# Fifteen low weight parts of the first mixer on GpSimd instead of VectorE

## The chip, the cores and the metric

One NeuronCore of a Trainium2 chip runs the whole program in one launch. The metric is device time in microseconds (us), the median over timed executions; lower is better. One further execution was taken by the hardware profiler, and all durations below come from that one. The engines are TensorE (PE, with its weight loads as PEld), VectorE (DVE), ScalarE (ACT), GpSimd (POOL) and SyncE (SP), each with its own instruction queue that runs strictly in order.

## What is computed

Two transformer-like blocks in fp32 on 256 tokens of width 1024, batch 1. The change concerns the first half of the first block, here called the first mixer:

```python
def first_block(x, ...):
    xn = rms_norm(x, norm1_w)
    z = xn @ w_in                       # q, k_c, v_c, k_s, v_s, k_w, v_w, g_nsa, xr, gr, g_a, g_b
    attn = nsa_attention(q, ...)        # compressed, selected and windowed keys, three softmaxes
    rnn = rg_lru_branch(xr, gr, ...)    # conv of 4, gated linear recurrence
    merged = sigmoid(g_a) * (attn @ w_up_attn) + sigmoid(g_b) * (rnn @ w_up_rnn)
    x = x + merged @ w_out
    hn = rms_norm(x, norm2_w)
    x = x + square(relu(hn @ mlp_w1)) @ mlp_w2
    return rms_norm(x, final_norm_w)

def compress_blocks(k, pos, w1, w2):    # k_c and v_c, blocks of 32 tokens with stride 16
    ...
    return gelu(flat @ w1) @ w2
```

The second block is a SwiGLU, a mixer with two attentions, and a second SwiGLU.

## The kernel before, in words

**Weights in pieces.** All weights lie in one DRAM tensor in the order of use. A piece is up to 1024 columns of 128 partitions (the first eight: 512). Two pieces make a chunk, which one DMA on the SP queue loads into a `raw` buffer (three buffers, `load_to`, L227 to L241). To keep fp32 accuracy with TensorE's fp32r format, each piece is split: ACT copies it to `whi`, rounded to fp32r (L253), and DVE subtracts, `wlo = raw - whi` (L254). `whi` and `wlo` have five buffers each. `wt` (L258) calls for a piece's split when the piece two ahead of it is needed. Each product of TensorE then takes three matmuls: `whi` with the high and the low part of the activations, and `wlo` with the high part (L305, L299).

Each buffer comes free when its last reader is done: a `raw` buffer when both `whi` and both `wlo` of its chunk are made, a `whi` or `wlo` buffer when TensorE has used it.

**What sets the order.** The code records steps in the order of `ORDER_1` (L156). A scheduler then places the instructions of each engine by its own estimate of durations and of what is ready; the result is a fixed list for every engine. An edit of one instruction's engine can thus change the lists of all engines.

**Pieces of the first mixer.** Pieces 0 to 68 belong to it: `q`, `k`, `xr`, `vg`, the gates `ga`, `gb`, `gr`, the compression weights `cw1` (pieces 16, 17, 18, 22, 23, 24, 27, 28), the recurrence `lru`, and the two merges `m1b` and `m1a`. From piece 69 on comes `wo`, the output projection. Names used below:

- `Sn`: attention scores (L825, L826), from `q` and from `k`, whose low part for the other half of the partitions is an ACT copy (L589).
- `cmpA`: the rows of `k_c` and `v_c`, shifted, written by four DMAs that GpSimd issues (L569, L570), first the two of group 0 and then the two of group 1. `cmpB` is their high and low part: eight ACT copies (L334) and eight DVE subtractions (L335), four for each group. `cmph` is the product of `cmpB` and the compression weights (L674); its first half needs four of the eight, two of each group.
- `vg`: values and gates (L299), first with piece 19.
- GpSimd's other work in this stretch is `rnn_prep`, a chain of some 25 operations on 128x8 elements (L886 to L905, a series for softplus), and `rs_A` (L476), the reciprocal root of the first norm.
- `rnn`: the recurrence's output in two parts, high by ACT (L334) and low by DVE (L335), which `m1b` multiplies (L305).

Of the kernel before, what the change touches and what calls it, by code (L numbers as in the profile page):

```python
# [8 lines left out]
F32 = mybir.dt.float32  # L9
F32R = mybir.dt.float32r  # L10
AF = mybir.ActivationFunctionType
ALU = mybir.AluOpType
# [11 lines left out]
EARLY = 8  # L24
# [164 lines left out]
class Prog:  # L189
# [15 lines left out]
    def prepare(self):  # L205
        self.chunks = self.plan.chunks()
        self.chunk_of = {}
        self.off = []
        o = 0
        for ci, ch in enumerate(self.chunks):  # L210
            w = sum(self.plan.pieces[i][0] for i in ch)
            self.off.append((o, w))
            o += P * w
            x = 0
            for i in ch:
                self.chunk_of[i] = (ci, x)
                x += self.plan.pieces[i][0]
        self.total = o
        self.raw = {}
        self.split = {}  # L220
        self.n_dma = 0
        self.n_split = 0
        self.hi_ins = []
        self.lo_ins = []
        self.raw_ins = []
# [17 lines left out]
    def split_to(self, i):  # L243
        nc = self.nc
        while self.n_split <= min(i, len(self.plan.pieces) - 1):
            p = self.n_split
            ci, x = self.chunk_of[p]
            self.load_to(ci + 2 if ci >= EARLY else max(ci + 2, EARLY))
            w = self.plan.pieces[p][0]
            src = self.raw[ci][:, x:x + w]  # L250
            hi = self.pools["whi"].tile([P, PIECE], F32R, tag="whi", name=f"whi{p}")
            lo = self.pools["wlo"].tile([P, PIECE], F32R, tag="wlo", name=f"wlo{p}")
            self.hi_ins.append(nc.scalar.activation(out=hi[:, :w], in_=src, func=AF.Copy))  # L253
            self.lo_ins.append(nc.vector.tensor_tensor(out=lo[:, :w], in0=src, in1=hi[:, :w].bitcast(F32), op=ALU.subtract))  # L254
            self.split[p] = (hi, lo)
            self.n_split += 1

# [1342 lines left out]
```

## Time and profile before

| what | value |
|---|---|
| median of 3 runs | 966.38 us (965.74 to 966.56) |
| profiled execution, its own time | 965.97 us |
| its span, first to last instruction | 964.2 us |
| instructions | 15723 |
| share of busy time | PE 98%, PEld 90%, DVE 75%, ACT 61%, POOL 4% |

The profiled execution lies 0.41 us below the median, and its span 1.8 us below its own time. A busy share is a mean over the whole program. What ends the idle time of an engine stands in brackets in a timeline's rows, and a row with a count (x2) merges instructions of the same kind that follow each other, so its time runs from the first start to the last end. The ends of matmuls are modelled: rows of PE overlap, and what counts is when the next one starts.

### The profile page before, as it was taken

The page shows a single profiled execution, that of the slowest core. Times are in us where ns is not written, and L with a number is a line of the kernel's source. Part 1 is how long each engine was busy: PE and PEld are TensorE (multiplying, and loading weights), DVE is VectorE, ACT ScalarE, POOL GpSimd, SP SyncE. Part 2 cuts the span into 40 slices and gives each one's busy share as a digit, 9 for nine tenths or more (in the row PEclk, how much of TensorE's full clock was granted, in tenths as well). Part 3 has the DMA queues.
Part 4 walks back from the last instruction along what each step waited for, and adds up shares of the span by engine and source line. Part 5 has one row for each costly group of instructions (what it writes and reads, how often), then busy time and mean ns, then how long its engine had stood idle before and what let it go on. Part 6 is the DMA issues. An engine that isn't in the chain of part 4 may idle for free.

```text
span 964.2 us, 15723 instructions
## 1 busy us (share of the span) xinstructions
PE 947.1 (98%) x6176; PEld 863.0 (90%) x6176; DVE 727.5 (75%) x1215; ACT 585.7 (61%) x962; POOL 36.6 (4%) x71
## 2 busy tenths in 40 slices
PE   7999999999999999999999999999999999999997
PEld 6989999998888888888888888999999888888885
DVE  6898879878887655579888666779776878878553
ACT  6695798546766544456555445588874566555541
POOL 1600000000000000020000200000000000000000
PEclk9999999999999999999999999999999999999999
DMA  8666333645555555556555755454333465554541
GB/s 302 218 229 250 130 135 132 228 139 185 180 198 190 175 181 201 186 189 196 197 193 178 234 189 178 142 196 140 124 123 141 175 233 182 189 204 173 179 159 44
DMA packets 27563, 174.01 MB, mean 180 GB/s; under 512 B 3425, under 2 KB 4705, under 8 KB 8289
## 3 DMA queue, kind: packets, MB, share of 16 engines
q1 hardware_dynamic: 25920, 169.60, 50.4%
q0 software_dynamic: 1136, 2.63, 1.2%
q8 instruction: 48, 0.79, 0.3%
q10 hardware_dynamic: 432, 0.79, 0.2%
q14 instruction: 27, 0.21, 0.1%
HBM read 171.43 MB, written 1.05 MB: 179 GB/s over the span
## 4 chain that ended last, share of the span: by engine, by line
PE 94%; ACT 3%; DVE 1%; issue 1%; DMA 1%; SPq 0%; POOLq 0%; POOL 0%; ACTq 0%; DVEq 0%
PE f L311 17%; PE w L311 12%; PE f L312 9%; PE w L312 6%; PE ld L299 6%; PE ga L305 5%; PE gb L305 5%; PE fd L311 4%; PE wo L311 3%; PE m1b L305 2%; PE gr L305 2%; PE fd L312 2%; PE xr L305 2%; PE wo L312 2%; PE qa L305 1%; PE m2b L305 1%
## 5 line engine op out<-in xcount | busy, mean ns | idle before, releaser
L254 DVE TENSOR_TENSOR wlo<-raw,whi 128x1024 fp32r<-128x1024 f32 (+2 forms) x324 | 388.7, 1203 | 167.2 <-ACT whi L253 147.6
L253 ACT ACTIVATE whi<-raw 128x1024 fp32r<-128x1024 f32 (+2 forms) x324 | 336.0, 1042 | 290.9 <-PE w L311 66.6
L311 PE MATMUL f<-u,whi 128*128 128x512 f32 x704 | 244.9, 393 | 0.0
L312 PE MATMUL f<-u,wlo 128*128 128x256 f32 x704 | 196.2, 279 | 0.0
L311 PEld LDWEIGHTS f<-u,whi 128*128 128x128 f32 x704 | 131.7, 187 | 29.7
L312 PEld LDWEIGHTS f<-u,wlo 128*128 128x128 f32 x704 | 132.7, 189 | 0.2
L311 PE MATMUL w<-hid,whi 128*128 128x512 f32 x256 | 90.5, 399 | 0.0
L311 PE MATMUL w<-u,whi 128*128 128x512 f32 x256 | 90.1, 398 | 0.0
L312 PE MATMUL w<-hid,wlo 128*128 128x256 f32 x256 | 71.9, 281 | 0.0
L312 PE MATMUL w<-u,wlo 128*128 128x256 f32 x256 | 71.5, 281 | 0.0
L311 PE MATMUL fd<-f1h,whi 128*128 128x512 f32 x176 | 61.1, 394 | 0.0
L311 PEld LDWEIGHTS w<-hid,whi 128*128 128x128 f32 x256 | 48.1, 188 | 12.1
L311 PEld LDWEIGHTS w<-u,whi 128*128 128x128 f32 x256 | 47.9, 188 | 11.5
L299 PE MATMUL ld<-whi,f2h 128*128 128x512 f32 x176 | 54.4, 390 | 0.0
L305 PE MATMUL ga<-u,whi 128*128 128x256 f32 x256 | 48.7, 286 | 1.2 <-ACT whi L253 1.2
L312 PE MATMUL fd<-f1h,wlo 128*128 128x256 f32 x176 | 48.8, 277 | 0.0
L305 PE MATMUL gb<-u,whi 128*128 128x256 f32 x256 | 48.7, 285 | 0.0
L312 PEld LDWEIGHTS w<-u,wlo 128*128 128x128 f32 x256 | 48.3, 189 | 0.2
L312 PEld LDWEIGHTS w<-hid,wlo 128*128 128x128 f32 x256 | 48.4, 189 | 0.0
L311 PE MATMUL wo<-m,whi 128*128 128x512 f32 x128 | 44.6, 395 | 0.0
L305 PEld LDWEIGHTS ga<-u,whi 128*128 128x128 f32 x256 | 40.2, 191 | 1.5 <-ACT whi L253 1.5
L305 PEld LDWEIGHTS gb<-u,whi 128*128 128x128 f32 x256 | 40.4, 191 | 0.1
(540 smaller groups left out, 1886.9 us busy)
## 6 DMA issues: line engine op xcount, KB each, us to landing
raw<-in_ws_dram SPq DMA_DIRECT2D x150, 1024.0 KB, 4.8
raw<-in_ws_dram SPq DMA_DIRECT2D x3, 960.0 KB, 4.8
raw<-in_ws_dram SPq DMA_DIRECT2D x2, 992.0 KB, 4.7
raw<-in_ws_dram SPq DMA_DIRECT2D x7, 256.0 KB, 5.3
nar<-in_rpb_dram POOLq DMA_DIRECT2D x16, 96.0 KB, 5.3
res<-in_x_dram SPq DMA_DIRECT2D x8, 128.0 KB, 4.8
raw<-in_ws_dram SPq DMA_DIRECT2D x1, 932.0 KB, 4.6
raw<-in_ws_dram SPq DMA_DIRECT2D x1, 768.0 KB, 4.5
```

Of the source, the lines that this page charges most:

```text
L253: self.hi_ins.append(nc.scalar.activation(out=hi[:, :w], in_=src, func=AF.Copy))
L254: self.lo_ins.append(nc.vector.tensor_tensor(out=lo[:, :w], in0=src, in1=hi[:, :w].bitcast(F32), op=ALU.subtract))
L299: mm(out, a, b, start=start and r == 0, stop=stop and r == 2, skip_group_check=True)
L305: mm(out, a, b, start=start and r == 0, stop=stop and r == 2, skip_group_check=True)
L311: mm(bank.rearrange("p (a t) -> p a t", a=2), wh, x, start=start, stop=False, skip_group_check=True)
L312: mm(bank[:, :T], wl, x[:, 0, :], start=False, stop=stop, skip_group_check=True)
```

## The change

`mixer_end` is the number of the first piece of `wo`, 69. For every fourth piece from 11 on, up to 67, the subtraction is issued on GpSimd. These are 15 of the 61 pieces that the first mixer splits after the first eight: 11, 15, 19, ..., 67. Fourteen have 1024 columns, piece 19 has 840.

```diff
@@ prepare
         self.total = o
+        self.mixer_end = self.plan.loc["wo", 0, 0][0]
@@ split_to
             self.hi_ins.append(nc.scalar.activation(out=hi[:, :w], in_=src, func=AF.Copy))
-            self.lo_ins.append(nc.vector.tensor_tensor(out=lo[:, :w], in0=src, in1=hi[:, :w].bitcast(F32), op=ALU.subtract))
+            eng = nc.gpsimd if p >= EARLY and p % 4 == 3 and p < self.mixer_end else nc.vector
+            self.lo_ins.append(eng.tensor_tensor(out=lo[:, :w], in0=src, in1=hi[:, :w].bitcast(F32), op=ALU.subtract))
```

The lists of all engines differ in the first mixer. In the rows below a name's first number is that of the piece (`wlo15` is the low part of piece 15), the last one only counts tiles; in the new code L254 stands at L256, and later lines are shifted by two.

GpSimd, before: the end of `rnn_prep`, then the DMAs of `cmpA`, and the gates.

```order
L902 TENSOR_TENSOR sp_w_785<-sp_w_785,sp_z_786 128x8
L904 TENSOR_SCALAR sp_w_785<-sp_w_785 128x8
L905 TENSOR_TENSOR rp_778<-sp_w_785,rp_778 128x8
L569 DMA cmpA_397<-kv_sb_395 64x512
L570 DMA cmpA_397<-kv_sb_395 64x2x255
L618 MEMSET v_1_677 128x4x64 x2
L640 COPY gateA_758<-gates_680 128x8 x3
```

GpSimd, now: the same place.

```order
L256 TENSOR_TENSOR wlo15_511<-raw11_323,whi15_510 128x1024
L904 TENSOR_TENSOR sp_w_785<-sp_w_785,sp_z_786 128x8
L906 TENSOR_SCALAR sp_w_785<-sp_w_785 128x8
L907 TENSOR_TENSOR rp_778<-sp_w_785,rp_778 128x8
L571 DMA cmpA_397<-kv_sb_395 64x512
L572 DMA cmpA_397<-kv_sb_395 64x2x255
L620 MEMSET v_1_677 128x4x64 x2
L256 TENSOR_TENSOR wlo19_652<-raw13_480,whi19_651 128x840
L256 TENSOR_TENSOR wlo23_732<-raw15_637,whi23_731 128x1024
L256 TENSOR_TENSOR wlo27_877<-raw17_707,whi27_876 128x1024
L642 COPY gateA_758<-gates_680 128x8 x3
```

The subtraction of piece 15 now stands ahead of the `cmpA` DMAs, and so does that of piece 11, near the start of `rnn_prep` (not shown); those of 19, 23 and 27 stand between the DMAs and the gates.

ScalarE, before: from piece 18 to piece 20. The first `cmpB` row reads group 0, the second group 1.

```order
L253 ACTIVATE whi18_639<-raw13_480 128x1024
L334 ACTIVATE cmpB_615<-cmpA_397 128x8x15 x4
L589 ACTIVATE k_1_468<-k_1_468 64x512
L253 ACTIVATE whi19_651<-raw13_480 128x840
L580 ACTIVATE q_1_402<-q1_538 64x512 x2
L334 ACTIVATE cmpB_615<-cmpA_397 128x8x15 x4
L253 ACTIVATE whi20_665<-raw14_545 128x840
```

ScalarE, now: the same place.

```order
L336 ACTIVATE cmpB_615<-cmpA_397 128x8x15 x4
L254 ACTIVATE whi18_639<-raw13_480 128x1024
L336 ACTIVATE cmpB_615<-cmpA_397 128x8x15
L591 ACTIVATE k_1_468<-k_1_468 64x512
L336 ACTIVATE cmpB_615<-cmpA_397 128x8x15 x3
L582 ACTIVATE q_1_402<-q1_538 64x512 x2
L254 ACTIVATE whi19_651<-raw13_480 128x840
L254 ACTIVATE whi20_665<-raw14_545 128x840
```

The copies of group 1 have moved up: one ahead of the copy of `k` (L591) and three ahead of `q` and `whi19`. Until the DMAs of group 1 have landed, all that stands behind the first of them waits.

TensorE, before: the first scores, then `vg` with piece 19.

```order
L825 MATMUL Sn000_826<-k_1_468,q_1_402 128x256
L825 MATMUL Sn001_827<-k_1_468,q_1_402 128x256
L826 MATMUL Sn000_826<-k_1_468,q_1_402 128x256
L299 MATMUL vg0_683<-whi19_651,u0_0_131 128x280
L299 MATMUL vg1_684<-whi19_651,u0_0_131 128x280
```

TensorE, now: the same place.

```order
L827 MATMUL Sn000_826<-k_1_468,q_1_402 128x256
L827 MATMUL Sn001_827<-k_1_468,q_1_402 128x256
L828 MATMUL Sn000_826<-k_1_468,q_1_402 128x256
L676 MATMUL cmph_636<-whi16_547,cmpB_615 64x256
L676 MATMUL cmph_636<-wlo16_548,cmpB_615 64x256
```

The 24 matmuls of `cmph` with pieces 16 to 18, which before stood behind `vg` with pieces 19 and the start of 20, now come ahead of `vg`.

## Rows read from the trace of the kernel before

**Rows 1.** The page, busy time, share of the span and instructions of each engine.

```profile
PE 947.1 (98%) x6176; PEld 863.0 (90%) x6176; DVE 727.5 (75%) x1215; ACT 585.7 (61%) x962; POOL 36.6 (4%) x71
```

**Rows 2.** Busy time by stretch: bounds, length, then each engine's busy us (instructions).

```profile
46.60:64.10 17.50, 14.97 (x112) 13.67 (x111) 16.13 (x44) 17.20 (x38) 0.00 (x0) 1.00 0.44 143
...
75.00:143.00 68.00, 68.00 (x569) 67.61 (x568) 56.33 (x134) 52.33 (x105) 0.00 (x0) 1.00 0.48 169
143.00:188.00 45.00, 45.00 (x370) 44.52 (x370) 44.57 (x98) 34.06 (x60) 0.00 (x0) 1.00 0.48 167
```

**Rows 3.** Timeline of PE, 46 to 65 us: start, duration, instruction, idle before and releaser.

```profile
46.64 0.41 PE L825 MATMUL Sn<-k,q 128*128 128x256 f32 x2
...
47.71 0.53 PE L299 MATMUL vg<-whi,u 128*128 128x280 f32 x2 [0.31 <-ACT whi L253]
...
62.09 0.50 PE L305 MATMUL ga<-u,whi 128*128 128x256 f32 x2 [1.23 <-ACT whi L253]
...
64.14 0.28 PE L305 MATMUL ga<-u,wlo 128*128 128x256 f32 x1
```

**Rows 4.** Timeline of POOL, 23 to 41 us, and one row of 608 us.

```profile
23.47 1.06 POOL L891 TENSOR_TENSOR rp<-rp 128x8 f32<-128x8 f32 x1 [3.15 <-ACT rp L273]
24.62 1.10 POOL L895 TENSOR_SCALAR sp_w<-rp 128x8 f32<-128x8 f32 x1
...
28.75 0.24 POOL L901 TENSOR_SCALAR sp_w<-sp_w 128x8 f32<-128x8 f32 x1
...
33.51 1.26 POOL L901 TENSOR_SCALAR sp_w<-sp_w 128x8 f32<-128x8 f32 x1
...
39.05 0.64 POOL L569 DMA_DIRECT2D cmpA<-kv_sb  x1
...
40.29 0.53 POOL L569 DMA_DIRECT2D cmpA<-kv_sb  x1
40.80 0.60 POOL L570 DMA_DIRECT2D cmpA<-kv_sb  x1
...
608.19 0.52 POOL L1335 MEMSET vahi<- 128x512 f32 x1
```

**Rows 5.** Timeline of DVE.

```profile
23.25 2.36 DVE L254 TENSOR_TENSOR wlo<-raw,whi 128x1024 fp32r<-128x1024 f32 x2
...
33.46 1.22 DVE L254 TENSOR_TENSOR wlo<-raw,whi 128x1024 fp32r<-128x1024 f32 x1
...
107.12 1.22 DVE L254 TENSOR_TENSOR wlo<-raw,whi 128x1024 fp32r<-128x1024 f32 x1
...
171.19 0.68 DVE L335 TENSOR_TENSOR rnn<-rg,rnn 128x512 fp32r<-128x512 f32 x1
```

**Rows 6.** Landing of the `cmpA` DMAs: line L569, then line L570, two DMAs each.

```profile
DMA to landing us min/median/max: 2.3/4.7/7.1
...
DMA to landing us min/median/max: 2.9/4.8/6.7
```

**Rows 7.** Timeline of ACT, 44 to 63 us.

```profile
44.75 1.33 ACT L334 ACTIVATE cmpB<-cmpA 128x120 fp32r<-128x120 f32 x4
46.10 0.63 ACT L589 ACTIVATE k<-k 64x512 fp32r<-64x512 f32 x1
46.75 0.91 ACT L253 ACTIVATE whi<-raw 128x840 fp32r<-128x840 f32 x1
...
48.34 1.29 ACT L580 ACTIVATE q<-q 64x512 fp32r<-64x512 f32 x2
...
60.99 1.04 ACT L253 ACTIVATE whi<-raw 128x1024 fp32r<-128x1024 f32 x1
```

**Rows 8.** Timeline of PE at 44, at 113 and at 172 us.

```profile
44.00 0.28 PE L305 MATMUL xr<-u,wlo 128*128 128x256 f32 x1
...
113.25 0.28 PE L305 MATMUL gr<-u,wlo 128*128 128x256 f32 x1
...
171.73 0.52 PE L305 MATMUL m1b<-rnn,whi 128*128 128x256 f32 x3
```

## The prediction

> **What bounds the kernel now.** The page comes first: PE is busy for 947.1 of 964.2 us [rows 1]. Some 17 us of it are idle in all, and an edit that only makes DVE freer can win no more than the part of them that lies where the edit works. So the second view is the busy time by stretch [rows 2]. From 75 to 143 us and from 143 to 188 us PE has no idle time at all, though DVE is nearly full in the second (44.57 of 45.00). Only from 46.6 to 64.1 us does PE stand still within the first mixer, for 17.50 - 14.97 = 2.53 us. The timeline names four gaps, the first 0.31 and the last 1.23 us, and each ends with a `whi` of ACT, none with a `wlo` of DVE [rows 3]. ACT is busy for 17.20 of the 17.50 us there [rows 2]: in this stretch ACT is the bound, and ACT's work is not made less by the change. So the gain is at most 2.53 us, if the new order fills these gaps, and whatever new wait PE gets is paid in full, because behind 64 us it has no gaps that could take it up.
>
> **The subtraction itself.** Fifteen subtractions leave DVE, 1.22 us each at 1024 columns [rows 5]: 18 us less for an engine that PE does not wait for. On GpSimd the trace has no such operation. From below, DVE's 1.22 us bounds it. Its nearest row is a MEMSET, 0.52 us for 512 columns written [rows 4]: two inputs read one after the other at that rate are 4 x 0.52 = 2.1 us for 1024, and two reads and a write, nothing overlapped, are 3.1. I take 2.1, since a write can go beside the reads; 840 columns are then 1.7.
>
> The Trainium skill (GPSIMD Engine Reference, Performance versus the Vector engine) gives 4497 ns for an add of 2048 fp32 columns; halved, as an estimate, 2.25 us. The sum below would then be some 0.4 us larger.
>
> GpSimd also waits for DVE. An operation on 128x8 takes 0.24 us alone; the one that began at 33.51 took 1.26 us, and DVE had begun a `wlo` at 33.46 that took 1.22. The two that began at 23.47 and 24.62 took 1.06 and 1.10, beside the pair of `wlo` that began at 23.25 [rows 4, 5]. So a moved piece can start up to 1.2 us late as well.
>
> **What is queued behind it on GpSimd.** This is the place that I think decides. GpSimd's list from 23.47 to the four `cmpA` DMAs (39.05 to 40.80) has no pauses to speak of [rows 4]. Pieces 11 and 15 are put into this list ahead of the DMAs. They add 2 x 2.1 = 4.2 us. Two holds fall away, since DVE no longer makes these two pieces: that of the operation at 24.62 (1.10 - 0.24 = 0.9) and that at 33.51 (1.26 - 0.24 = 1.0) [rows 4]. The DMAs leave 4.2 - 1.9 = 2.3 us later. Bounds: 2 x 1.22 - 1.9 = 0.5, and 2 x 3.1 - 1.9 + 1.2 = 5.5.
>
> The first two DMAs landed 2.3 and 2.9 us after their issue, the last two 7.1 and 6.7 us [rows 6], at 40.29 + 7.1 = 47.4 and 40.80 + 6.7 = 47.5. I keep the 6.7, since weight loads will run beside them again: group 1 lands at L = 40.80 + 2.3 + 6.7 = 49.8. Before, ACT wanted group 1 only after both copies of `k`, `whi19` and `q`, later than 48.34 + 1.29 = 49.6, and so waited for nothing. Now it stands right behind group 0 and `whi18`, and ACT has done those, in either order, by 44.75 + 1.33 = 46.1 [rows 7]. The change thus turns a hidden DMA into a wait of ACT of 3.7 us, in the one stretch where PE hangs on ACT.
>
> **What PE does then**, from L on:
> - The first score matmuls are done at about 46.9 [rows 3]; the next needs the copy of `k`, which ends one `cmpB` (1.33 / 4 = 0.33) and 0.63 us behind L [rows 7]: L + 1.0.
> - `cmph` needs three more `cmpB` copies (1.0) and DVE's last part of it (about 0.3): L + 2.3. PE has 0.3 us of scores before it and waits 1.0 us.
> - `whi19` ends 1.0 + 1.29 + 0.91 us behind the copy of `k` [rows 7], at L + 4.2, and PE is then still busy with `cmph`, as 24 matmuls at 0.115 us last to L + 5.1. But `wlo19` comes from GpSimd at L + 4.2 + 1.7 + up to 1.2, while PE wants it near L + 5.7: a wait of 0.2 to 1.4, taken as 0.6. Piece 23 stands closer to its use than DVE's were, another 0 to 1.0, taken as 0.3.
> - The work itself: from 46.9 to 64.14, less 2.53 of gaps, 14.7 us [rows 2, 3].
>
> Sum: L + 1.0 + 14.7 + 1.0 + 0.6 + 0.3 = L + 17.6 = 67.4, for the place that before came at 64.14. ACT does not come later than that: it worked from 46.10 to 60.99 + 1.04 without rest, 15.9 us, so its `whi25` is there near L + 16 [rows 7]. **The change costs 3.2 us here**, the 2.53 of gaps already given back within it.
>
> **The rest of the mixer.** For the other pieces I take nothing. Piece 15 is wanted at 44.00 [rows 8] and ready near 40 to 41, by the queue above. Pieces 27 and 31 are split while PE is already late, which gives them 3 us more. Of those from 35 to 67 the tightest by far, 59 apart, is 43: made at 107.12 + 1.22 = 108.34 and wanted at 113.25 [rows 5, 8], 4.9 us, which covers 2.1 - 1.22 = 0.9 and a hold of 1.2. Piece 59 was late only because DVE was full, and GpSimd's queue passes that by. PE stays dense, so the 3.2 us reach the end. Profiled span: 964.2 + 3.2 = 967.4. The median lies 0.41 us above the profiled execution's own time (965.97), so on the median of 966.38 the forecast is **969.6 us**, 0.33% slower. (About 0.2%, 1.9 us, is what a measurement of this kernel can tell from no change.)
>
> **Rivals.**
> *A. The late DMAs cost little.* The 6.7 and 7.1 us are nearly three times the landing of the first two, so it may be a weight load that the last two waited for, and their landing may not depend on when they are issued. With L = 47.5 as before, the sum is 65.1: 1.0 us slower. With a landing of 2.9 us [rows 6], 40.80 + 2.3 + 2.9 = 46.0, ACT waits for nothing and the sum is 63.6: 0.5 us faster. For it speaks the spread of the landings; against it that GpSimd's lateness also holds the `raw` buffer of pieces 14 and 15, so a weight load of its own moves onto the DMAs. 965.9 to 967.4 us, no change that can be told.
>
> *B. DVE is held up by GpSimd, where DVE is full.* Four moved pieces (51, 55, 59, 63) fall into 143 to 188 us. If GpSimd holds DVE off for its 2.1 us each time, DVE loses 4 x (2.1 - 1.22) = 3.5 us there, where it has 0.43 us of rest [rows 2]. The place where this decides is `rnn`: DVE's part began at 171.19 and took 0.68, and PE took it at 171.73 [rows 5, 8], with nothing between. Each us that DVE then comes later is PE's, up to 3.5 on top of 3.2: 973.1 us. For it: holds in one direction are in the rows above. Against it: much of DVE's work there reads PSUM, the four pieces themselves leave DVE's queue, and the new order makes `rnn` earlier in it.
> The Trainium skill (SBUF — State Buffer, Who interferes with whom) has the rule: GpSimd and a VectorE instruction with two inputs in SBUF exclude each other for a whole instruction, whichever starts first. By that, B would come in full; the rows show only the short operations of GpSimd being held, never DVE.
>
> *C. Faster.* `cmph` now stands ahead of `vg`, where PE waited for `whi19` and `whi20`. If `cmpB` of group 1 were made by 46, these matmuls would fill the gaps, at best all 2.53 us: 963.9 us. Four copies take 1.33 us [rows 7], so it needs DMAs that land by 44.7, 2.8 us earlier than before, though they leave later.
>
> **How the numbers follow.** Forecast 0.50, A 0.30, B 0.15, C 0.05. The forecast's own range, from the bounds of the DMAs' delay (0.5 to 5.5) and of the two waits (0.2 and 0 to 1.4 and 1.0), runs from 967.1 to 974.3; a tenth of it falls short of 1.9 us. Slower by over 0.2%: 0.45 of the forecast and all of B, and the edges of A taken as none: 0.60. Within 0.2%: A and 0.05 of the forecast, 0.35. Faster: C, 0.05. The range from 966.0 to 974.0 leaves out C, the lower edge of A, and B together with a late forecast, about 2 in 10.
>
> **What would show it.** Right: in the new profile the `cmpA` DMAs leave GpSimd 2 to 3 us later, ACT has a wait of some 2 to 4 us before a `cmpB` near 46 us that a DMA ends, and PE a gap of 3 us or more before the scores' L828 at 47. PE's gaps between 46 and 68 sum to 3.9 + 1.0 + 0.6 + 0.3 = 5.8 us in place of 2.5. GpSimd's subtractions take near 2.1 us. Wrong: those DMAs on time, or PE's gaps there below 2.5 us (A, C); or gaps of PE behind 140 us that end with DVE (B), with DVE's `wlo` or `rnn` longer than 1.22 and 0.68 us.

## The result, and the profile after

The changed kernel takes **974.00 us** (median of 4 runs, 973.70 to 974.14) against 966.27 us (4 runs, 965.74 to 966.56): a ratio of 1.0078 with a 95% interval of 1.0063 to 1.0093, 7.7 us slower. The profiled execution has 972.2 us of span, before 964.2. The direction and the first cause were forecast; the size, 3.2 us, was less than half of what came, and 974.00 us lies on the upper edge of the stated range.

The first lines of the page, as in [rows 1]:

```profile
PE 949.6 (98%) x6176; PEld 865.4 (89%) x6176; DVE 735.4 (76%) x1200; ACT 586.2 (60%) x962; POOL 76.6 (8%) x86
...
PEclk8999999999999999999999999999999999999999
```

Fifteen subtractions left VectorE, some 18 us in all, and yet it is busy for 7.9 us longer than before. TensorE is busy for 2.5 us longer with the same 6176 matmuls.

Busy time by stretch (columns as in [rows 2]; behind the five engines the granted clock), the three stretches of [rows 2] with the one between them, and then the part of the first stretch in which TensorE comes back to work:

```profile
46.60:64.10 17.50, 13.04 (x91) 12.64 (x90) 14.33 (x35) 15.50 (x34) 3.78 (x2) 0.90 0.48 171
64.10:75.00 10.90, 8.85 (x69) 7.93 (x68) 10.90 (x17) 9.60 (x18) 3.67 (x2) 1.00 0.63 218
75.00:143.00 68.00, 67.89 (x563) 67.25 (x562) 60.60 (x130) 52.05 (x102) 15.72 (x10) 1.00 0.52 183
143.00:188.00 45.00, 43.30 (x358) 42.79 (x357) 44.79 (x96) 35.20 (x65) 11.27 (x4) 1.00 0.45 155
50.00:52.30 2.30, 0.48 (x3) 0.49 (x4) 1.00 (x3) 1.54 (x4) 0.00 (x0) 0.97 0.00 0
52.30:55.00 2.70, 2.70 (x15) 2.70 (x14) 2.48 (x6) 2.63 (x6) 0.02 (x1) 0.50 0.00 0
55.00:57.00 2.00, 2.00 (x17) 2.00 (x16) 1.81 (x8) 1.98 (x4) 2.00 (x1) 0.86 0.00 0
```

Most of the loss has two places. One is 46.6 to 75 us. The other is 143 to 188 us, where TensorE had no idle time before and now has 1.70 us.

**The first place, the queue.** The timeline of GpSimd, as in [rows 4] (two moved pieces and the four `cmpA` DMAs), then of ScalarE, as in [rows 7], then of TensorE, as in [rows 3]:

```profile
23.42 3.35 POOL L256 TENSOR_TENSOR wlo<-raw,whi 128x1024 fp32r<-128x1024 f32 x1 [3.06 <-DVE acc L503]
...
38.01 2.41 POOL L256 TENSOR_TENSOR wlo<-raw,whi 128x1024 fp32r<-128x1024 f32 x1
...
42.42 0.64 POOL L571 DMA_DIRECT2D cmpA<-kv_sb  x1
43.05 0.62 POOL L572 DMA_DIRECT2D cmpA<-kv_sb  x1
43.65 0.53 POOL L571 DMA_DIRECT2D cmpA<-kv_sb  x1
44.16 0.60 POOL L572 DMA_DIRECT2D cmpA<-kv_sb  x1
```

```profile
42.30 0.38 ACT L336 ACTIVATE cmpB<-vec 128x32 fp32r<-128x32 f32 x2
47.04 1.33 ACT L336 ACTIVATE cmpB<-cmpA 128x120 fp32r<-128x120 f32 x4 [4.36 <-DMA cmpA<-kv_sb]
48.28 1.04 ACT L254 ACTIVATE whi<-raw 128x1024 fp32r<-128x1024 f32 x1
50.71 0.40 ACT L336 ACTIVATE cmpB<-cmpA 128x120 fp32r<-128x120 f32 x1 [1.39 <-DMA cmpA<-kv_sb]
51.13 0.63 ACT L591 ACTIVATE k<-k 64x512 fp32r<-64x512 f32 x1
```

```profile
51.81 0.39 PE L828 MATMUL Sn<-k,q 128*128 128x256 f32 x1 [4.42 <-ACT k L591]
...
65.42 0.33 PE L676 MATMUL cmph<-wlo,cmpB 128*64 128x256 f32 x1 [0.32 <-POOL wlo L256]
68.11 0.38 PE L307 MATMUL ga<-u,wlo 128*128 128x256 f32 x1 [0.17 <-DVE wlo L256]
72.80 0.38 PE L307 MATMUL ga<-u,wlo 128*128 128x256 f32 x1 [1.44 <-DVE wlo L256]
```

The DMAs leave 3.4 us later than in [rows 4]. ScalarE waits for both groups, 4.36 and 1.39 us, and TensorE stands still for 4.42 us before the scores. Behind this gap its granted clock is 0.50 of full speed, 1.2 of 2.4 GHz, until 55.6 us; the 0.86 of the last row above is a mean of both levels. In the last two rows above, 2.70 us of work at half speed and 2.00 at 0.86 are 1.35 + 0.28 = 1.6 us lost, as an estimate that takes a matmul at half the clock as twice as long (the `cmph` matmuls start 0.21 us apart there, and 0.11 to 0.13 us apart behind 55.6 us).

The weight loads beside these DMAs came later too. Issues of weight loads on SyncE's queue near 35 and 40 us, before and after:

```profile
34.70 0.33 SPq L237 DMA_DIRECT2D raw<-in_ws_dram  x1
...
40.49 0.33 SPq L237 DMA_DIRECT2D raw<-in_ws_dram  x1
```

```profile
40.45 3.57 SPq L238 DMA_DIRECT2D raw<-in_ws_dram  x2
```

The row of after holds two issues, at 40.45 and 43.69 us. The load that left at 34.70 now waits for the `raw` buffer of pieces 14 and 15, and so for GpSimd's subtraction of piece 15, which ends at 38.01 + 2.41 = 40.42. Two weight loads now run beside the `cmpA` DMAs.

**The second place, the holding.** VectorE at 69 us and at 172 us, then GpSimd at the same times, then what TensorE waits for at 175 us:

```profile
69.44 3.30 DVE L256 TENSOR_TENSOR wlo<-raw,whi 128x1024 fp32r<-128x1024 f32 x1
...
172.02 3.35 DVE L256 TENSOR_TENSOR wlo<-raw,whi 128x1024 fp32r<-128x1024 f32 x1
```

```profile
69.26 2.40 POOL L256 TENSOR_TENSOR wlo<-raw,whi 128x1024 fp32r<-128x1024 f32 x1 [3.89 <-ACT whi L254]
...
170.77 3.51 POOL L256 TENSOR_TENSOR wlo<-raw,whi 128x1024 fp32r<-128x1024 f32 x1 [12.13 <-ACT whi L254]
```

```profile
176.88 0.35 PE L827 MATMUL Sn<-k,q 128*128 128x256 f32 x1 [1.70 <-DVE nmn L787]
```

A `wlo` of VectorE that takes 1.22 us alone [rows 5] takes 3.30 and 3.35 us: it ends 1.1 us, its own length, behind the end of GpSimd's. It works in the other direction as well: the piece that began at 170.77 took 3.51 us, since VectorE was at work on two `rnn` when it started. Beside 14 of the 15 moved pieces an operation of VectorE is stretched so. TensorE's row shows the price of the second: `nmn` stands behind this `wlo` in VectorE's list.

Where the lateness is, from the timelines of TensorE: the end of the `ga` matmuls of piece 26 near 70 us, the end of the last `m1b` matmul near 199 us, and the span (us; in brackets the difference to before). The rows below the second belong to the experiments.

| kernel | `ga`, piece 26 | `m1b`, last | span |
|---|---|---|---|
| before | 69.93 | 198.68 | 964.2 |
| changed | 75.68 (+5.8) | 206.78 (+8.1) | 972.2 (+8.0) |
| 11 and 15 alone | 76.31 (+6.4) | 205.47 (+6.8) | 972.3 (+8.1) |
| 19 and later alone | 72.07 (+2.1) | 203.66 (+5.0) | 969.1 (+4.9) |
| all, DMAs first | 71.18 (+1.3) | 202.29 (+3.6) | 967.7 (+3.5) |
| 11 and 15, DMAs first | 69.93 (0) | 199.10 (+0.4) | 965.9 (+1.7) |
| without 19, 27, 59, DMAs first | 69.58 (-0.4) | 199.38 (+0.7) | 965.5 (+1.3) |
| late DMAs, nothing moved | 74.72 (+4.8) | 203.48 (+4.8) | 969.0 (+4.8) |

### The profile page after: what moved, and what is told of

The parts are those of the page before. It is cut to its first block, busy times and chain, and to the rows that moved or that the text cites. A ratio compares the mean times of both kernels' runs of the same rounds, so it can differ in the third digit from the quotient of the medians.

```text
span 972.2 us, 15737 instructions
## 1 busy us (share of the span) xinstructions
PE 949.6 (98%) x6176; PEld 865.4 (89%) x6176; DVE 735.4 (76%) x1200; ACT 586.2 (60%) x962; POOL 76.6 (8%) x86
## 4 chain that ended last, share of the span: by engine, by line
PE 88%; DVE 7%; ACT 2%; issue 1%; DMA 1%; SPq 0%; POOLq 0%; POOL 0%; ACTq 0%; DVEq 0%
PE f L313 17%; PE w L313 12%; PE f L314 9%; PE w L314 6%; PE ld L301 6%; PE fd L313 4%; PE ga L307 4%; PE wo L313 3%; DVE wlo L256 2%; PE gb L307 2%; PE m1b L307 2%; PE xr L307 2%; PE fd L314 2%; PE wo L314 2%; PE qa L307 1%; PE m2b L307 1%
## 5 line engine op out<-in xcount | busy, mean ns | idle before, releaser
L254 ACT ACTIVATE whi<-raw 128x1024 fp32r<-128x1024 f32 (+2 forms) x324 | 336.2, 1042 | 286.9 <-PE w L313 69.1
L256 DVE TENSOR_TENSOR wlo<-raw,whi 128x1024 fp32r<-128x1024 f32 (+2 forms) x309 | 377.5, 1225 | 167.4 <-ACT whi L254 149.2
L256 POOL TENSOR_TENSOR wlo<-raw,whi 128x1024 fp32r<-128x1024 f32 (+1 forms) x15 | 42.0, 2801 | 106.5 <-ACT whi L254 76.6
```

The lines of the kernel that those rows point to most:

```text
L256: self.lo_ins.append(eng.tensor_tensor(out=lo[:, :w], in0=src, in1=hi[:, :w].bitcast(F32), op=ALU.subtract))
```

## The experiments

Two theories. **Queue**: the subtractions of pieces 11 and 15 stand ahead of the `cmpA` DMAs in GpSimd's list, and the late DMAs make the stall at 47 to 52 us. **Holding**: GpSimd's subtraction holds an operation of VectorE until it is over, and where the held operation is the next that TensorE wants, TensorE waits. The rival to both is that the new order of the instructions is bad by itself.

### Pieces 11 and 15 alone

```diff
-            eng = nc.gpsimd if p >= EARLY and p % 4 == 3 and p < self.mixer_end else nc.vector
+            eng = nc.gpsimd if p >= EARLY and p in (11, 15) else nc.vector
```

> Only pieces 11 and 15, the two that stand ahead of the cmpA DMAs in GpSimd's list, stay on GpSimd; the other thirteen go back to VectorE. ScalarE's order is the same as with all fifteen (a copy of group 1 ahead of the copy of k). Queue theory (the late DMAs make the stall): the DMAs leave near 42.4 us again, TensorE stands still for about 4.4 us before the scores near 51 us and its granted clock is 0.5 behind that; no gap that ends with VectorE behind 64 us. The first ga matmul with wlo comes near 67.6 in place of 64.1, and the time is 966.3 + 4 = about 970.3. Rival (GpSimd and VectorE hold each other off, and that is where the time goes): these two pieces cost under 1 us, about 967.

Measured: 973.88 us (971.15 to 974.07, 5 runs; before 966.56), ratio 1.0070 [1.0058, 1.0083]. Two pieces cost as much as fifteen. TensorE's gaps, and the busy time from 64 to 75 us and from 70 to 72 us:

```profile
52.06 0.39 PE L828 MATMUL Sn<-k,q 128*128 128x256 f32 x1 [4.77 <-ACT k L591]
66.58 0.51 PE L307 MATMUL ga<-u,whi 128*128 128x256 f32 x2 [0.60 <-ACT whi L254]
68.97 0.33 PE L676 MATMUL cmph<-whi,cmpB 128*64 128x256 f32 x1 [1.06 <-ACT whi L254]
```

```profile
64.10:75.00 10.90, 9.24 (x64) 8.74 (x63) 10.37 (x21) 9.46 (x18) 0.00 (x0) 0.84 0.85 310
70.00:72.00 2.00, 2.00 (x11) 2.00 (x11) 2.00 (x5) 2.00 (x4) 0.00 (x0) 0.50 0.86 348
```

The gap is there without the thirteen others, so the queue makes it. The 4 us expected of it were too few: ScalarE, the bound here, has lost some 6 us by waiting and stays late, so that TensorE waits for `whi` again at 66 and 69 us, and behind that the clock is at 0.50 a second time. At the `ga` matmuls of piece 26 this kernel is 0.6 us later than the changed one (table): there the changed kernel has its hold of 1.44 us, and this one has lost as much to ScalarE's lateness and the clock. From there on the changed kernel loses 2.3 us more by 199 us. This one loses 0.4 us there and 1.3 us between 209 and 219 us, where the changed one loses nothing (more on that below, with the DMAs first). That both end 8 us late is in part chance.

Once more, for the spread:

> The run with only pieces 11 and 15 on GpSimd once more, for its spread: its five times went from 971.15 to 974.07 us, and in the profiled execution (974.07) the granted clock was at 0.50 twice, at 52 to 55 us and again at 70 to 72 us. If the second fall is what parts the fast from the slow executions, an execution near 971 to 972.5 has the first fall only, and one at 974 has both. If all executions have both, the spread has another cause.

Measured: 972.74 us (971.93 to 974.66, 6 runs), ratio 1.0063 [1.0051, 1.0075]. The profiled execution was again a long one (973.83 us) and had both falls of the clock. What the executions near 971 to 972 us lack was not seen, and stays open.

### Pieces 19 and later alone

```diff
-            eng = nc.gpsimd if p >= EARLY and p % 4 == 3 and p < self.mixer_end else nc.vector
+            eng = nc.gpsimd if p >= 19 and p % 4 == 3 and p < self.mixer_end else nc.vector
```

> The thirteen pieces from 19 on stay on GpSimd; 11 and 15 go back to VectorE, so that nothing new stands ahead of the cmpA DMAs, and ScalarE's order there is that of the kernel before. Queue theory: the DMAs leave near 39 to 41 us, no stall at 47 to 51 us, the clock stays at 1.00. Holding theory: VectorE's wlo26 near 66 us and an operation near 172 us still take 2.4 to 3.4 us beside a GpSimd subtraction, TensorE still has gaps of 1 to 2 us that end with VectorE, and the time is 974.0 - 4 = about 970. If the queue were all of it, 966.3.

Measured: 970.88 us (970.67 to 971.33, 5 runs; before 966.56), ratio 1.0048 [1.0035, 1.0060]. GpSimd's first `cmpA` DMA, and TensorE's longest gap of the mixer:

```profile
39.15 0.64 POOL L571 DMA_DIRECT2D cmpA<-kv_sb  x1
```

```profile
173.78 0.36 PE L827 MATMUL Sn<-k,q 128*128 128x256 f32 x1 [1.75 <-DVE nmn L787]
```

The DMAs are on time, the stall and the fall of the clock are gone, and 4.3 us remain. The gap at 174 us is that of the changed kernel to 0.05 us. So the holding is a cost of its own.

### All fifteen, the DMAs first

```diff
-            nc.gpsimd.dma_start(out=src[64:128, g, :, 0:T - 1], in_=kv3[64 * g:64 * g + 64, :, 1:T])
+            S["cmp_dma"] = nc.gpsimd.dma_start(out=src[64:128, g, :, 0:T - 1], in_=kv3[64 * g:64 * g + 64, :, 1:T])
...
-            nc.gpsimd.tensor_scalar(out=w, in0=w, scalar1=1.0 / k, scalar2=None, op0=ALU.add)
+            ins = nc.gpsimd.tensor_scalar(out=w, in0=w, scalar1=1.0 / k, scalar2=None, op0=ALU.add)
+            if k == 17:
+                G.behind(ins, S["cmp_dma"])
```

> All fifteen pieces stay on GpSimd, but the long chain of small operations (from the loop over k on) is ordered behind the four cmpA DMAs, so that these leave as soon as piece 15 is subtracted, near 36 to 38 us in place of 42.4 to 44.2. ScalarE's order from 36 to 50 us is that of the changed kernel. Queue theory: ScalarE waits for no DMA, TensorE's gap of 4.4 us before the scores and the fall of the clock are gone, and the time is 974.0 - 4 = about 970, or down to 968.5 if the gaps of the kernel before fill as well. If the new order of ScalarE (group 1 ahead of k), and not the DMAs' issue, makes the stall: 973 to 974. The gaps behind 64 us that end with VectorE stay by either theory.

Measured: 969.93 us (969.52 to 970.24, 5 runs; before 966.56), ratio 1.0037 [1.0024, 1.0051]. GpSimd's first `cmpA` DMA; ScalarE's first copy of group 1; TensorE's longest gaps:

```profile
35.96 0.64 POOL L571 DMA_DIRECT2D cmpA<-kv_sb  x1
```

```profile
46.17 0.40 ACT L336 ACTIVATE cmpB<-cmpA 128x120 fp32r<-128x120 f32 x1
```

```profile
52.93 0.40 PE L301 MATMUL vg<-wlo,u 128*128 128x280 f32 x1 [1.21 <-POOL wlo L256]
...
68.29 0.38 PE L307 MATMUL ga<-u,wlo 128*128 128x256 f32 x1 [1.31 <-DVE wlo L256]
...
172.40 0.36 PE L827 MATMUL Sn<-k,q 128*128 128x256 f32 x1 [1.73 <-DVE nmn L787]
```

The same fifteen subtractions, the same order on ScalarE to 80 us, and 4.1 us less: the new order is not what stalls ScalarE, the lateness of the DMAs is. What is left are three waits of 4.2 us together: one for a subtraction on GpSimd itself (piece 19), two for VectorE held beside pieces 27 and 59.

### Pieces 11 and 15, the DMAs first

The two edits above together.

> Only pieces 11 and 15 on GpSimd, as in the run that took 973.88 us, but with the cmpA DMAs ordered before the chain of small operations. ScalarE's order is the same in both. Queue theory: the DMAs leave near 36 to 38 us, ScalarE and TensorE wait for none of them, the granted clock stays at 1.00 from 47 to 75 us, and the whole 7.3 us are gone: 966 to 967. If the order of ScalarE's work (three copies of group 1 ahead of q and whi19, more pieces split ahead) is bad by itself, the later gaps at 66 and 69 us stay: 967.5 to 969.

Measured: 968.35 us (967.46 to 968.90, 11 runs; before 966.31), ratio 1.0020 [1.0011, 1.0029]. Of the 7.3 us of the two pieces 2.0 stay. In the mixer nothing is left (table: 0 at 70 us, 0.4 at 199 us); the rest, 1.3 us, arises between 209 and 219 us, at the first `wo` matmuls, as it does in the run with late DMAs and these two pieces. GpSimd has no subtraction there, but the lists differ. `m` is what the first `wo` matmul reads. In both runs VectorE works through three `tga` of `m1a` before its first part of `m`, where the kernel before has two and the changed one has one. First the kernel before, then this run:

```profile
207.37 0.69 DVE L335 TENSOR_TENSOR m<-tga,m 128x512 fp32r<-128x512 f32 x1
```

```profile
209.93 0.68 DVE L337 TENSOR_TENSOR m<-tga,m 128x512 fp32r<-128x512 f32 x1
```

```profile
210.76 0.47 PE L313 MATMUL wo<-m,whi 128*128 128x512 f32 x1 [0.15 <-DVE m L337]
```

`m` begins 2.6 us later than before, though TensorE is only 0.4 us late at 199 us, and the matmul starts when it is done. From there to 215 us VectorE has no rest, and TensorE starts late three times more, by 0.1 to 0.3 us. So the rival to both theories, the new order by itself, has a share here. It is read from the lists; no run puts only this order back.

### Without pieces 19, 27 and 59, the DMAs first

```diff
+            eng = nc.gpsimd if p >= EARLY and p % 4 == 3 and p < self.mixer_end and p not in (19, 27, 59) else nc.vector
```

> As the run with the cmpA DMAs first (969.93 us), but pieces 19, 27 and 59 go back to VectorE; twelve stay on GpSimd. In that run TensorE's three longest waits behind 46 us were for these: 1.21 us for wlo19 itself, 1.31 us for VectorE's wlo26 held beside piece 27, and 1.73 us for nmn behind VectorE's wlo58 held beside piece 59, 4.2 us together. If the holding of VectorE costs only where a held operation is the next that TensorE wants, the twelve others cost next to nothing, though VectorE is held beside each of them: 969.9 - 4.2 = 965.7, no slower than before. If the cost lies in the busy time of VectorE as such (some 1 us more per moved piece), it shrinks with the number of pieces, 15 to 12: 969.2 or so.

Measured: 967.21 us (965.94 to 967.48, 11 runs; before 966.31), ratio 1.0006 [0.9996, 1.0015]. Three pieces out of fifteen carry 2.7 of the remaining 3.4 us; the twelve others cost 0.9 us, which can't be told from nothing. Pieces 11 and 15 are among the twelve, and alone they cost 2.0 us: the order of `m` that makes 1.3 us of that is not in this kernel's lists. So holding as such is nearly free; what it costs is decided by what is held.

### Piece 59 alone

```diff
+            eng = nc.gpsimd if p == 59 else nc.vector
```

> One piece alone, 59, on GpSimd; all else is the kernel before. Holding theory: VectorE's wlo58 takes some 3.3 us beside it near 165 us, nmn comes 1.7 us later than TensorE wants it, and the time is 966.5 + 1.7 = 968.2. If that wait is one of a late and crowded schedule only (with all fifteen moved), one piece hides: 966.5.

Measured: 966.54 us (965.39 to 966.93, 11 runs; before 966.31), ratio 0.9998 [0.9989, 1.0007]: the rival was right, one piece hides. The subtraction on GpSimd, and the operation of VectorE that it holds:

```profile
165.50 2.76 POOL L256 TENSOR_TENSOR wlo<-raw,whi 128x1024 fp32r<-128x1024 f32 x1 [91.58 <-ACT whi L254]
```

```profile
166.96 1.84 DVE L979 TENSOR_TENSOR rg<-xc,rg 128x512 f32<-128x512 f32 x1
168.73 1.22 DVE L256 TENSOR_TENSOR wlo<-raw,whi 128x1024 fp32r<-128x1024 f32 x1
```

With the other pieces back, the order on VectorE is another one: an `rg` is held, 1.84 us in place of 0.68, which TensorE doesn't want soon, and no `wlo` with `nmn` behind it. A price per piece can't be given from the piece.

### GpSimd reads one input

```diff
-            self.lo_ins.append(eng.tensor_tensor(out=lo[:, :w], in0=src, in1=hi[:, :w].bitcast(F32), op=ALU.subtract))
+            if eng is nc.gpsimd:
+                self.lo_ins.append(eng.tensor_scalar(out=lo[:, :w], in0=hi[:, :w].bitcast(F32), scalar1=0.0, scalar2=None, op0=ALU.mult))
+            else:
+                self.lo_ins.append(eng.tensor_tensor(out=lo[:, :w], in0=src, in1=hi[:, :w].bitcast(F32), op=ALU.subtract))
```

> As the changed kernel, but GpSimd writes the high part times 0.0 in place of source minus high part: one input is read, not two. This leaves the low part of these fifteen pieces out (the time of a matmul doesn't hang on values). If reading two inputs at once is what holds VectorE off, VectorE's operations beside the fifteen keep their own times (wlo 1.22 us, and no gap at 72 and 177 us), and the time is 974.0 - 4 = 970 or less, the operation being shorter too. If any GpSimd operation on SBUF of this length holds VectorE, its operations are stretched for as long as GpSimd's lasts: with about half the length, 1.2 us, half of the holding cost remains, 971 to 973, and the queue is 2 x 1.2 us shorter as well.

Measured: 964.78 us (964.00 to 966.29, 10 runs; before 966.56), ratio 0.9983 [0.9974, 0.9992]. In this kernel the order changed as well: the first DMA leaves at 38.99 us, and group 1 stands behind the copy of `k` again, so it says nothing on the queue. On the holding it does. Two of GpSimd's operations, and what VectorE did beside the first and the second:

```profile
64.75 2.77 POOL L257 TENSOR_SCALAR wlo<-whi 128x1024 fp32r<-128x1024 f32 x1 [4.19 <-ACT whi L254]
```

```profile
105.59 2.78 POOL L257 TENSOR_SCALAR wlo<-whi 128x1024 fp32r<-128x1024 f32 x1 [11.92 <-DVE cmpsum L759]
```

```profile
65.65 1.23 DVE L259 TENSOR_TENSOR wlo<-raw,whi 128x1024 fp32r<-128x1024 f32 x1 [0.60 <-ACT whi L254]
```

```profile
105.66 0.99 DVE L847 TENSOR_TENSOR fn<-fn,gateA 128x6 f32<-128x6 f32 x1
```

```profile
107.54 0.91 DVE L765 TENSOR_TENSOR cmpf<-cmprc,gates 128x8 f32<-128x8 f32 x2
```

The operation is longer than the subtraction (2.77 against 2.40 us) and holds VectorE for less: an operation that starts with it is held until some 1.1 us behind its start, and a `wlo` that starts 0.9 us behind runs at its own 1.23 us within it. Some small operations near its end are held again, to its end: each of the two `cmpf` in the last row takes 0.17 us alone. Neither theory had this; it lies between the two expectations. From 64 to 215 us TensorE has no gap at all. The time, 1.8 us below the kernel before, is no gain, since the low part of fifteen pieces is left out. So the holding for a whole length belongs to the subtraction with two inputs. The edit changed the kind of instruction along with the number of inputs, and which of the two counts was not shown.

### Late DMAs, nothing moved

```diff
+        for _ in range(11):
+            nc.gpsimd.tensor_scalar(out=w, in0=w, scalar1=1.0, scalar2=None, op0=ALU.mult)
         nc.gpsimd.tensor_scalar(out=ta, in0=ta, scalar1=0.0, scalar2=-8.0, op0=ALU.max, op1=ALU.mult)
```

> The kernel before, all low parts on VectorE, with eleven more small multiplications by 1.0 on 128x8 (0.31 us apart) in GpSimd's chain ahead of the cmpA DMAs: these leave some 3.4 us later, near 42.5 us, as in the changed kernel, but ScalarE keeps the old order (group 1 behind k, whi19, k and q). If the lateness alone makes the loss: ScalarE waits for group 0 until about 47 us, 2.3 us more than before, TensorE pays a gap of 4 us or more, the clock falls, and the time is 970 to 974. If the order of ScalarE counts as much as the lateness: group 1, which lands near 50.6 us, is not waited for (it is wanted near 51.9 us), the gap is 2.3 to 2.6 us and the time 968 to 969.

Measured: 970.73 us (968.81 to 970.98, 5 runs; before 966.38), ratio 1.0036 [1.0024, 1.0048]. The eleven operations took 6.15 us, not 3.4, so the DMAs leave 7.2 us late. GpSimd, ScalarE and TensorE:

```profile
46.24 0.63 POOL L569 DMA_DIRECT2D cmpA<-kv_sb  x1
```

```profile
49.61 1.29 ACT L334 ACTIVATE cmpB<-cmpA 128x120 fp32r<-128x120 f32 x4 [4.63 <-DMA cmpA<-kv_sb]
```

```profile
51.60 0.58 PE L826 MATMUL Sn<-k,q 128*128 128x256 f32 x1 [4.42 <-ACT k L589]
```

A gap of 4.42 us and a fall of the clock (0.50 from 51.1 to 57.8 us, twice as long as in the changed kernel), with all low parts on VectorE: late DMAs alone make them. That the two gaps are equal is chance: here ScalarE waits once, for group 0 of DMAs that are 7.2 us late, in the changed kernel twice, for DMAs that are 3.4 us late. What 3.4 us cost in the old order was not measured. The delay was twice that of the changed kernel and the loss 4.3 us, less than the 7.3 us of pieces 11 and 15, of which 1.3 us arise behind 209 us. So the place of the copies on ScalarE matters too: in the new order it takes them up at 42.7 us, with `whi18` behind them, in the old one `whi18` comes first and group 1 is not waited for. And landing is not tied to issue: these DMAs land 2.3 to 2.8 us behind their issue, beside no weight load, those of the changed kernel up to 6.6 us behind theirs, beside two, and group 1 is there near 50.7 us in both.

### Two other uses of GpSimd, on the kernel before

Copies with one input in place of ScalarE, which bounds 46.6 to 64.1 us: the high parts of pieces 20 and 21,

```diff
+            if p in (20, 21):
+                self.hi_ins.append(nc.gpsimd.tensor_scalar(out=hi[:, :w], in0=src, scalar1=1.0, scalar2=None, op0=ALU.mult))
+            else:
...
```

> Another use of GpSimd, on the kernel before: it makes the high parts of pieces 20 and 21 (copies with one input, 840 and 560 columns) in place of ScalarE, and VectorE keeps all low parts. From the run in which GpSimd read one input, a copy of 840 columns takes 2.33 us and holds VectorE under 1 us. ScalarE, which bounds 46.6 to 64.1 us, loses 0.9 + 0.6 us of work there, so that TensorE's gaps for whi22 and whi25 (0.42 and 1.23 us) go and perhaps that at 51.8 us (0.43): 1.5 to 2 us less, about 964.7. If instead the slower copy comes late for its own matmuls (vg near 51.4 us) or its hold delays wlo19, nothing is won: 966.5 or above.

Measured: 965.42 us (964.70 to 968.31, 11 runs; before 966.31), ratio 0.9992 [0.9983, 1.0000]. And, with the DMAs first, all eight `cmpB` copies of `cmp_x`:

```diff
...
+                        hh = h[:, g, sl, 0:15]
+                        nc.gpsimd.tensor_scalar(out=hh, in0=src[:, g, :, a:a + 15], scalar1=1.0, scalar2=None, op0=ALU.mult)
+                        nc.vector.tensor_tensor(out=l[:, g, sl, 0:15], in0=src[:, g, :, a:a + 15], in1=hh.bitcast(F32), op=ALU.subtract)
...
```

> Another use of GpSimd, from what the runs so far showed: the cmpA DMAs first, and then GpSimd, in place of ScalarE, makes all eight cmpB copies (one input, 128x120 each); all low parts stay on VectorE. ScalarE loses 8 x 0.33 = 2.7 us of work ahead of and within 46.6 to 64.1 us, where it bounds the kernel. If ScalarE is the only bound there, most of TensorE's 2.5 us of gaps go: 964 to 964.5. If VectorE (16.1 of 17.5 us busy there) or the place of the copies in GpSimd's list becomes the bound, nothing is won: 966 or above.

Measured: 965.30 us (964.76 to 966.87, 11 runs; before 966.38), ratio 0.9990 [0.9982, 0.9999]. Both are about 1 us below the kernel before, at the edge of what can be told and between the times that the two theories of each gave, and well below the changed kernel. In both, TensorE's gaps for `whi` shrink and gaps for VectorE (`cmpB`, `nmn`, 0.7 and 1.1 us) take their place: VectorE is the next bound of this stretch.

## Why the prediction was right, and where it was not

- **The number**: the range ended at 974.0, and its text put a late forecast together with rival B outside it. Just that came; that 974.00 us still lies on the edge of the range is luck. The prediction's own signs say the same: those of the queue came (DMAs 3.4 us late, a gap of 4.42 us before the scores), and so did the sign of rival B that it had listed under "wrong".
- **What bounds the kernel**: ScalarE decides from 46 to 64 us, as said; the two other uses, which relieve it there, come out about 1 us lower. That a freer VectorE wins nothing was not tested, since VectorE did not become freer. TensorE does stand still once more in the first mixer, for 4.38 us up to 9.19 us, ahead of the pieces at issue; this bears on the clock alone (last section).
- **The subtraction**, 2.1 us: 2.37 to 2.41 us where nothing holds it, 2.80 on the mean with holds. The estimate from the Trainium skill (GPSIMD Engine Reference, Performance versus the Vector engine), 2.25 us, was nearer than the one from the memset.
- **The DMAs' delay**, 2.3 us (0.5 to 5.5): 3.4. The two pieces took 3.35 + 2.41 = 5.8 us in place of 4.2; 2.4 us of holds fell away, net, in place of 1.9.
- **Landing of group 1**, L = 49.8: ScalarE's wait for it ended at 50.71. The landing time taken over (6.7 us) was good for the changed kernel (6.5), and the reason stands in the argument against rival A: weight loads moved beside the DMAs. Rival A's doubt was sound, its conclusion was not.
- **ScalarE's wait**, 3.7 us: 5.75, in two parts. That group 0 would be late as well was missed: the sum let ScalarE do it and `whi18` by 46.1, though the order printed ahead of the prediction shows `whi18` now behind the copies. This is the term most mis-sized in the stretch.
- **TensorE's gaps**: 3.9 us before the scores, measured 4.42; 1.0 at `cmph`, measured none; 0.6 and 0.3 for `wlo19` and `wlo23`, measured none and 0.32. **The clock** was no term at all: 1.6 us, more than the three small waits together (0.3 measured, 1.9 expected). Their sums nearly meet, 67.4 forecast and 68.11 measured for the `ga` matmul with `wlo25`, so the step gives the right end for partly wrong reasons.
- **"For the other pieces I take nothing"**: wrong, and this is where the forecast fell short. From 68 us on another 4 us are lost: 1.44 at 72 us, 1.70 at 177 us and smaller ones. The reasons given hold for the moved pieces, none of which TensorE waits for behind 68 us; it waits for what VectorE kept and was held at, a term put at nothing. Rival B named the mechanism and one of its places (143 to 188 us, 1.7 us there in place of up to 3.5; that at 72 us it did not have), and said that it would come on top, 973.1 us; it got a chance of 0.15. It decided not at `rnn` but at the `wlo` behind it. The first argument against it, that much of VectorE's work reads PSUM, is true of single operations (in the changed kernel the `attn` from `Sn` runs in its own 0.28 us within a subtraction of GpSimd at 55.7 us) but there is enough that reads SBUF: 14 of 15 pieces hold one.
- The rule of the Trainium skill (SBUF — State Buffer, Who interferes with whom), that a VectorE instruction with two SBUF inputs and a GpSimd one that reads SBUF exclude each other for a whole instruction, whichever starts first, stood against the change and was set aside as not shown by the rows. The trace agrees with it for the subtraction, 3.30 and 3.35 us in place of 1.22. It does not for the operation with one input, which reads SBUF too: within it a `wlo` ran at its own 1.23 us, so the rule is wider than what was measured. The rows of before had shown one direction of it; a lock seen from one side should have been priced from both.
- A part of the 8.0 us of the profiled executions is not the change's: the changed kernel's ran its first 25 us at a clock of 0.86, that of before at 1.00, 0.35 us at 46 us. Both values occur among the other runs: of the thirteen profiled executions, the six at 0.86 (piece 59 alone is one) are 0.3 to 0.8 us later at 46 us than that of before, and the seven at 1.00 (late DMAs are one) lie within 0.3 us of it.

## What to carry to other kernels

Before work goes to an idle engine, list what is queued behind it there, its DMAs above all, and what buffer its lateness keeps: two moved operations ahead of four DMAs cost 7.3 us, nearly as much as all fifteen. Look at whether an operation of one engine holds those of the other: here the engine that was to be relieved was busier afterwards. And price a stall on the bound engine with the fall of the clock behind it, and don't add two losses in one stretch where the later wait covers the earlier. An edit that only moves instructions can also change the lists far behind it: here that made 1.3 us.

## What the runs showed of the hardware that was not expected

- GpSimd's subtraction with two SBUF inputs (2.40 us at 1024 columns) holds a `wlo` of VectorE for its whole length, and a small one just as long: a TENSOR_SCALAR on 128x2 at 143 us, 0.15 us elsewhere, took 2.37. A longer operation with one input (2.77 us) holds one that starts with it for about 1 us, and some small ones near its end for up to 0.8 us; a `wlo` between them ran at its own 1.23 us.
- After a gap of TensorE of 4.4 to 4.8 us the granted clock was at 0.50 for 3 us or more, in the changed kernel and in each kernel with late DMAs; after gaps of up to 1.88 us behind 46 us it mostly stayed at 1.00, in the kernel before among them [rows 3]. The length of the gap does not settle it: in every profiled execution TensorE has a gap of 3.6 to 4.4 us that ends near 9 us, and the clock fell to 0.50 there, for some 6.8 us, in six of the thirteen. In that of before it stayed at 1.00 (its rows, then a stretch of the changed kernel's):

```profile
9.19 0.55 PE L1039 MATMUL kcvc<-u,whi 128*128 128x256 f32 x1 [4.38 <-DVE u L468]
```

```profile
7.80:14.60 6.80, 5.53 (x24) 5.27 (x25) 6.36 (x14) 5.41 (x12) 0.00 (x0) 0.50 1.05 389
```

With pieces 11 and 15 alone it fell a second time after gaps of 0.60 and 1.06 us; with the DMAs first the same two pieces had gaps of 0.49 and 1.06 us there, and it stayed at 1.00. Why it fell in the one and not in the other is open.
- Eleven operations of GpSimd on 128x8 in a row took 6.15 us, 0.56 each, while one alone takes 0.24 [rows 4]. Five of them took 0.23 or 0.24 us, and six 0.52 to 1.10 us, each of those beside an operation of VectorE with two inputs (a `wlo`, `xcp`, two `q` and two `k`). That the lengthening is holding was not tested.
